# A merge gate as the first unit of tile 0, and all head norms of tile 0 turned by VectorE

## The chip, the cores and the metric

The kernel runs on one core of one Trainium2 chip. The metric is the device time of one execution in microseconds (us), as the median of several runs. Lower is better.

## The reference

The kernel computes one layer of a hybrid decoder block on x of 2048 tokens and 1024 channels, all in float32. Cut to what matters here:

```python
h = rms_norm(x, norm_g)
u = einsum('bsd,dc->bsc', h, w_in)          # 1024 -> 8704 columns
v_c, b_c, c_c, z_c, q, k, v, z_a, gate_logits = split(u)
y_c = b_c * causal_conv3(c_c * v_c) * silu(z_c)
y_a = y_c @ w_conv_out
q, k = rms_norm(q per head of 64), rms_norm(k per head of 64)   # 16 query heads, 4 key heads
o = sliding_window_attention(q, k, v, sinks) * silu(z_a)        # window 128, blocks of 128
y_b = o @ w_attn_out
g_a, g_b = split(sigmoid(gate_logits + gate_b))
out = x + (g_a * y_a + g_b * y_b) @ w_out
```

The queries need an RMS norm per head of 64 channels before the attention, which asks for a sum of squares over those channels. The merge gates g_a and g_b need nothing but h; they are used only when y_a and y_b are merged.

## The kernel before, in words

The 2048 tokens are cut into two tiles of T = 1024 (t = 0 and 1), and each tile into two halves q of 512. Channels lie on the 128 partitions, tokens along the free dimension. A weight matrix is handled in units of 256 output columns: `q0` to `q3` are the queries (one unit is one key head with its four query heads), `cv0` to `cv7` the pairs (conv C, conv v), `b0` to `b3` conv B, `ga0` to `ga3` and `gb0` to `gb3` the merge gates, `z`, `za` the SiLU gates, `ya`, `yb` the two branch projections. `SEQ0` and `SEQ1` are the written-out orders of the units in the two tiles; a `+` joins two units that run interleaved. After tile 1 come eight units of the output projection.

Each float32 operand is split into a high and a low part, and a product is three matmuls (high by high, high by low, low by high) for each of four chunks: 12 matmuls of 128x512. An ordinary unit (`sunit`) is a 2x2x2 block product in seven such products instead of eight; it needs sums of operands (the forms 5, 6, 7 and 4) and sums of weights. The plain unit (`qunit`, kind "P" in the weight plan) takes eight products with the raw operands 1, 2, 8 and 3, so it can start while the sums are still being made. It yields its four results of 128x512 straight in PSUM banks, one after each second product. In the kernel before, `q0` of tile 0 is the one plain unit; it comes first behind the keys and values.

The order of work is written out by hand. Each product is one tick; `run` emits the product of a tick on TensorE and then what was put at that tick with `put(n, f)`. Thus the instruction stream of every engine and DMA queue follows the ticks, and each instruction waits only for the data or the buffer it needs. Tile 0 has 16 ticks for keys and values, then 8 for the plain unit, then 7 for every ordinary unit. `OP_X`, `OP_F`, `OP_S`, `OP_K` and so on hold ticks of the preparation at the front. `AT0` and `AT1` hold the 32 ticks at which the attention blocks (key head j, block b) of a tile begin; each block goes through loads on SP's queue five ticks ahead, scores (TensorE), exponent (ScalarE), normalising and a 32x32 turn (VectorE), a round trip through DRAM on POOL's queue, masks on POOL, values (TensorE) and an output store, over 15 ticks. `STATS_AT` is the tick at which the rows of tile 1's x begin to be loaded (eight transfers of 512 KB on POOL's queue, two ticks apart, `h_stats`, L1372) for tile 1's norm. The unit `z0` of tile 0 and all that follows it keeps its tick.

The norm of the queries (`fin_q`, from L811): each of the four results of a unit is copied to SBUF (L582), scaled and split into `q_h` and `q_l` (`parts`, L850 and L262) and stored to DRAM through POOL's queue (L855). Its sum of squares is taken from a turned copy: with `BY_PE[j]` 1 four TensorE transposes (L708) put tokens on the partitions; with 0 VectorE's STREAM_TRANSPOSE turns the 32x32 blocks. ScalarE squares the turned bank (L782) and VectorE reduces it. After VectorE's turn a head's sum lies in two parts in different partition groups, and `squares_sum` joins them by four ScalarE copies (L802) and four VectorE adds (L804) for a unit. The inverse root of `q0` to `q2` of tile 0 uses a Sqrt activation (`ROOT`, L279). The banks for the turned copies come from one pool of three PSUM banks (`mbank`), shared with the turned keys (`pbk`, L766) and the attention's values (`po`, L1116).

The merge gate (`fin_g`, L1191): one Tanh activation for each result, to be stored to DRAM by SP's queue (L1193).

Of the kernel before, what the change touches and what calls it, by code (L numbers as in the profile page):

```python
# [60 lines left out]
Q_PARTS = [1, 4, 4, 0]  # L61
Q_SUMS = [8, 7, 6, 3]
ROOT = (1, 1, 1, 0)
BY_PE = [1, 1, 1, 0]
OP_X = [1, 1, 1, 6, 7, 7, 8, 11]
OP_P = [3, 2, 3, 4, 4, 4, 5, 6]
OP_L = [7, 8, 6, 6, 8, 7, 9, 7]
# [4 lines left out]
OP_S = [15, 16, 16, 19, 21, 17, 23, 23, 20, 19, 22, 22, 27, 21, 23, 28]  # L72
OP_K = [11, 12, 18, 22, 8, 13, 20, 32, 15, 31, 26, 28, 39, 36]
SEQ0 = (
    "q0 q1 q2 q3 cv0 cv1 cv2 cv3 b0 cv4 cv5 b1 b2 cv6 cv7 b3 ga0 gb2 gb1 ga2 gb0 ga1 gb3 ga3 z0 "
    "z1 z2 z3 za0 za1 za2+za3 ya0+ya1 ya2+ya3 yb0+yb1 yb2+yb3")
SEQ1 = (
    "ga0+ga1 k q0 v q1 q2 cv0 q3 cv1 cv2 b0 cv3 ga3 b1 cv4 cv5 cv6 b2 cv7 gb1 b3 gb3 ga2 gb0 "
    "gb2 z0 z1 z2 z3 za0 za1 za2+za3 ya0+ya1 ya2+ya3 yb0+yb1 yb2+yb3")
STATS_AT = 115  # L80
ORDER = (1, 5, 6, 2, 7, 3, 4)
PAIR_PIECES = ((0, 0), (0, 1), (1, 0), (1, 1), (0, 2), (1, 2), (0, 3), (1, 3))
SUM_AT = {5: 0, 6: 1, 7: 2, 4: 3}
# [10 lines left out]
H_UP = 3  # L94
SUM_WAIT = 6
AT0 = [
    51, 56, 62, 66, 72, 78, 82, 87, 93, 99, 103, 108, 113, 119, 123, 127, 130, 135, 139, 142, 146, 149,
    153, 156, 160, 164, 167, 170, 174, 177, 181, 184]
AT1 = [
    41, 48, 56, 61, 67, 72, 75, 81, 84, 87, 90, 96, 99, 105, 109, 115, 119, 123, 126, 129, 132, 138,  # L100
    141, 144, 147, 150, 154, 157, 161, 164, 168, 174]
# [4 lines left out]
def block_kernel(  # L106
# [37 lines left out]
    def x_bank(name):  # L144
        return ps_x.tile([P, H], F32, tag="x", name=name)
# [385 lines left out]
    def qunit(key, ops, fin):  # L531


        u = unit(key)
        nm = "_".join(str(i) for i in key)
        for q in range(2):
            for i in range(2):
                ps = x_bank(f"Q{nm}_{i}_{q}")
                for p in range(2):
                    force(u, (i, p))  # L540
                    hi, lo = ready[u][i, p]
                    for j in range(KP):
                        b = ops[B_AT[p, q]][j]
                        for k, (w, m) in enumerate(((hi, 0), (hi, 1), (lo, 0))):
                            nc.tensor.matmul(
                                ps, lhsT=w[:, j, :], rhs=b[:, m, :],
                                start=p == 0 and j == 0 and k == 0, stop=p == 1 and j == KP - 1 and k == 2)
                    if p:
                        fin(i, q, ps)
                        live[0] -= 2 * q  # L550
                    yield
# [132 lines left out]
    def run(gen):  # L684
        while True:
            tick[0] += 1
            if next(gen, gen) is gen:
                tick[0] -= 1
                return
            hi, lo = (piece() if tick[0] >= W_FROM else None) or (None, None)  # L690
            if hi:
                hi()

            fs = at.pop(tick[0], [])
            for f in fs[:3]:
                f()
            if lo:
                lo()
            for f in fs[3:]:
                f()  # L700
            ahead_loads()
            vec.some(WOVEN)
# [105 lines left out]
    def fin_q(t, j):  # L808
        by_pe = t == 0 and BY_PE[j]
        ss = small.tile([P, 32 if by_pe else 64], F32, tag="ss" if by_pe else "ss4", bufs=3 if by_pe else 2, name=f"qss{t}_{j}")  # L810
# [629 lines left out]
    for t in range(NT):  # L1440
        def s(key, *srcs):
            plan.append(("S", srcs, key))

        def at_(key, c0):
            s(key, (w_in2, c0), (w_in2, c0 + P))

        if t == 0:
            for i in range(2):
                plan.append(("R", wkv[i * H : (i + 1) * H], ("kv", i)))
        for word in (SEQ0, SEQ1)[t].split():  # L1450
            both_ = word.split("+")
            for name in both_:
                if len(both_) > 1:
                    paired.add(len(plan))
                key, j = name.rstrip("0123456789"), int(name[-1]) if name[-1].isdigit() else None
                if key in ("ya", "yb"):
                    w = w_co if key == "ya" else w_ao
                    s((key, t, j), (w, j * UC), (w, j * UC + P))
                elif key == "cv":
                    s((key, t, j), (w_in2, COL_C + j * P), (w_in2, COL_V + j * P))  # L1460
                elif j is None:
                    at_((key, t), COLS[key])
                else:
                    at_((key, t, j), COLS[key] + j * UC)
                if t == 0 and name == "q0":
                    plan[-1] = ("P",) + plan[-1][1:]
    for n in range(S // P // 2):
        t, c0 = divmod(2 * n * P, T)
# [13 lines left out]
    raw, ops, xs = st["raw"], st["ops"], st["x"]  # L1482
# [171 lines left out]
    for t in range(NT):  # L1654
        ops = state[t]["ops"]
        ys, opa, opb = {}, {}, {}
        t0 = tick[0] + 1 if t else 1
        a0 = t0 + (14 if t else 0)
        attention(t, [a0 + n for n in (AT0, AT1)[t]])

        def unit_of(name, at_of):
            key, j = name.rstrip("0123456789"), int(name[-1]) if name[-1].isdigit() else None
            o = {"ya": opa, "yb": opb}.get(key, ops)
            if key == "k":
                return (key, t), o, fin_k(t)
            if key == "v":
                return (key, t), o, fin_v(t)
            if key == "q":
                fin = fin_q(t, j)
            elif key == "cv":  # L1670
                fin = fin_cv(t, j, ys)
            elif key == "b":
                fin = fin_b(t, j, ys)
            elif key in ("ga", "gb"):
                fin = fin_g(t, int(key == "gb"), j)
            elif key == "z":
                fin = fin_z(t, j, lambda k, q: yd[t][k, :, hs(q)], "z", ("c", t), ycd[t], at_of, nc.sync)
            elif key == "za":
                fin = fin_z(t, j, lambda k, q: od[t][k, :, hs(q)], "za", ("a", t), ocd[t], at_of, nc.gpsimd)
            else:  # L1680
                fin = fin_y(t, int(key == "yb"), j, at_of)
            return (key, t, j), o, fin

        if t + 1 < NT:
            h_stats(t + 1, tick[0] + STATS_AT)
        for word in (SEQ0, SEQ1)[t].split():
            n = tick[0] + 1
            if word == "z0":
                (h_prep if t + 1 < NT else w_prep)(*((t + 1,) if t + 1 < NT else ()), tick[0])
            if word == "za2+za3":  # L1690
                load_set(("c", t), n, opa)
            if word == "ya2+ya3":
                load_set(("a", t), n, opb)
            if word == "yb2+yb3":
                load_set(("h", t + 1) if t + 1 < NT else ("w", 0), n, x_state(t + 1)["ops"])
            names = word.split("+")
            if len(names) > 1:
                paired_units([
                    unit_of(name, lambda e, i=i, n=n: n + 2 * e + i) for i, name in enumerate(names)])
            elif t == 0 and word == "q0":  # L1700
                run(qunit(("q", 0, 0), ops, fin_q(0, 0)))
            else:
                run(sunit(*unit_of(word, lambda e, n=n: n + e)))

# [57 lines left out]
```

## Time and profile before

| | |
|---|---|
| median of 3 runs | 1891.03 us (1890.13 to 2689.12) |
| the profiled execution | 1891.0 us, span 1889.3 us |
| TensorE (PE) busy | 1880.3 us of the span, 8638 matmuls |
| VectorE (DVE) busy | 1540.2 us |
| ScalarE (ACT) busy | 988.9 us |
| GpSimd (POOL) busy | 726.6 us |
| granted TensorE clock | 1.0 |

A row of the profile names engine, line of the kernel, operation, `out<-in` by the program's tile names, shapes and count; then busy time, mean duration, and the idle time before with what ended it. PEld is the load of TensorE's stationary operand and overlaps PE. Matmuls overlap each other, so their rate is read from the distance between starts and not from a duration.

### The profile page before, as it was taken

Reading aid. Unit: us, or ns where it says so; the run is one execution under the profiler, and the core shown is the slowest. Engines: PE = TensorE matmul, PEld = TensorE weight load, DVE = VectorE, ACT = ScalarE, POOL = GpSimd, SP = SyncE. Lnnn points to the kernel's source line nnn. Section 1 sums busy time; section 2 is a strip of 40 time slices with the busy share of each in tenths; the row PEclk is TensorE's granted clock in tenths of the full one; section 3 lists DMA queues with packets and bytes.
Section 4 is the critical chain, followed back from the end, with each engine's and each line's share of the span. In section 5 each row is a group of like instructions: output and inputs, shape, how many; then the busy total and the mean of one; then the engine's idle time right before and its main releaser. Section 6 shows DMA issues by size and latency. Waiting matters only on the chain.

```text
span 1889.3 us, 27890 instructions
## 1 busy us (share of the span) xinstructions
PE 1880.3 (100%) x8638; PEld 1564.8 (83%) x8638; DVE 1540.2 (82%) x2536; ACT 988.9 (52%) x1993; POOL 726.6 (38%) x1038
## 2 busy tenths in 40 slices
PE   9999999999999999999999999999999999999999
PEld 7888888888888888888887888888888888888887
DVE  7989888789878889887588988888888779887654
ACT  7655554567665345435455645556566436444321
POOL 1472454466767111021075445656666311121000
PEclk9999999999999999999999999999999999999999
DMA  8475566689889978899367557768888879989653
GB/s 307 119 216 171 145 177 189 183 247 301 249 250 256 315 266 308 286 282 300 112 181 221 182 172 206 205 165 236 251 237 259 266 245 339 326 270 282 223 173 110
DMA packets 261188, 435.81 MB, mean 231 GB/s; under 512 B 33648, under 2 KB 124784, under 8 KB 261040
## 3 DMA queue, kind: packets, MB, share of 16 engines
q1 hardware_dynamic: 202848, 314.13, 50.6%
q0 software_dynamic: 58048, 119.87, 24.0%
q8 instruction: 69, 1.13, 0.2%
q14 instruction: 79, 0.65, 0.1%
q10 hardware_dynamic: 144, 0.03, 0.0%
HBM read 279.48 MB, written 154.42 MB: 230 GB/s over the span
## 4 chain that ended last, share of the span: by engine, by line
PE 91%; DVE 4%; DMA 3%; issue 1%; POOL 1%; ACT 1%; SPq 0%; POOLq 0%; DVEq 0%; ACTq 0%
PE Y L480 32%; PE Vcv L480 5%; PE Xcv L480 5%; PE s L1027 3%; PE Xz L480 2%; PE Xb L480 2%; PE Vb L480 2%; PE Vga L480 2%; PE Xga L480 2%; PE Vz L480 2%; PE Xza L480 2%; PE Vo L480 2%; PE Xo L480 2%; PE Xyb L480 2%; PE Vyb L480 2%; PE Vza L480 2%
## 5 line engine op out<-in xcount | busy, mean ns | idle before, releaser
L1078 POOL DMA_DIRECT2D x<-fd x256 | 143.8, 609 | 71.7 <-DMA fd<-f 37.1
L1099 POOL TENSOR_SCALAR_AFFINE_SELECT xh<-xh 64x512 fp32r<-64x512 f32 x64 | 66.7, 1042 | 134.8 <-DVE xl L262 98.5
L1051 ACT ACTIVATE p<-s,st,rq 128x128 f32<-128x128 f32 x256 | 113.0, 451 | 3.4 <-DMA fd<-f 2.7
L1071 POOL DMA_DIRECT2D fd<-f x64 | 38.6, 603 | 177.5 <-DVE f L262 162.8
L480 PE MATMUL Xcv<-oph,wcv_ah 128*128 128x512 f32 x256 | 79.1, 390 | 0.0
L1132 POOL DMA_DIRECT2D od<-o x64 | 69.3, 1090 | 21.0 <-ACT wz_d L362 8.0
L855 POOL DMA_DIRECT2D q2d<-q_h x64 | 44.3, 692 | 84.1 <-ACT q_h L850 81.9
L1322 POOL DMA_DIRECT2D md<-thyb x32 | 27.4, 872 | 100.1 <-DVE thyb L262 87.2
L1099 POOL TENSOR_SCALAR_AFFINE_SELECT xl<-xl 64x512 fp32r<-64x512 f32 x64 | 62.9, 983 | 4.4
L1099 POOL TENSOR_SCALAR_AFFINE_SELECT yp<-xl 64x512 fp32r<-64x512 f32 x64 | 55.9, 874 | 3.1
L1099 POOL TENSOR_SCALAR_AFFINE_SELECT yp<-yp 64x512 fp32r<-64x512 f32 x64 | 55.3, 863 | 4.2
L480 PEld LDWEIGHTS Xcv<-oph,wcv_ah 128*128 128x128 f32 x256 | 47.6, 188 | 9.4
L262 DVE SCALAR_TENSOR_TENSOR y<-u,cols,y 128x512 f32<-128x512 f32 x64 | 51.5, 804 | 3.7 <-ACT y L1161 2.5
L262 DVE TENSOR_TENSOR opa<-ina,opa 128x512 fp32r<-128x512 f32 x56 | 36.2, 686 | 21.6 <-ACT opa L297 21.4
L262 DVE TENSOR_TENSOR p<-p,st 128x512 f32<-128x512 f32 x64 | 49.2, 769 | 2.8
L1051 ACT ACTIVATION_READ_ACCUMULATOR p<-s,st,rq 128x1 f32 x256 | 51.1, 199 | 0.0
L362 ACT CAST wcv_sh<-wcv_raw 128x1024 fp32r<-128x1024 f32 x16 | 16.8, 1052 | 63.4 <-DVE wcv_raw L262 63.4
L480 PE MATMUL Xcv<-oph,wcv_al 128*128 128x512 f32 x128 | 49.9, 390 | 0.0
L855 POOL DMA_DIRECT2D q2d<-q_l x64 | 44.1, 689 | 13.6 <-DVE q_l L262 8.9
L262 DVE STREAM_TRANSPOSE f<-p 128x512 f32<-128x512 f32 x64 | 45.4, 710 | 2.6 <-DVE p L262 0.2
L262 DVE TENSOR_TENSOR opc<-inc,opc 128x512 fp32r<-128x512 f32 x56 | 36.1, 686 | 13.8 <-ACT opc L297 11.5
L480 PE MATMUL Y<-oph,wcv_d 128*128 128x512 f32 x192 | 46.4, 390 | 0.0
(774 smaller groups left out, 6594.4 us busy)
## 6 DMA issues: line engine op xcount, KB each, us to landing
wcv_raw<-in_w_in SPq DMA_DIRECT2D x32, 512.0 KB, 4.2
q<-q2d SPq DMA_DIRECT2D x64, 256.0 KB, 4.8
v<-vd SPq DMA_DIRECT2D x128, 128.0 KB, 4.4
fd<-f POOLq DMA_DIRECT2D x64, 256.0 KB, 3.8
x<-fd POOLq DMA_DIRECT2D x256, 64.0 KB, 3.5
gd<-th SPq DMA_DIRECT2D x64, 256.0 KB, 3.3
wq_raw<-in_w_in SPq DMA_DIRECT2D x16, 512.0 KB, 5.1
q2d<-q_h POOLq DMA_DIRECT2D x64, 128.0 KB, 3.6
```

Source lines behind the costliest of these rows:

```text
L262: r = f(*args, **kw)
L362: return (lambda: nc.scalar.copy(hi, src), lambda: vec.tensor_tensor(out=lo, in0=src, in1=hi.bitcast(F32), op=ALU.subtract))
L480: nc.tensor.matmul(ps, lhsT=w[:, j, :], rhs=b[:, m, :], start=start and j == 0 and i == 0, stop=j == KP - 1 and i == 2, skip_group_check=n ...
L855: nc.gpsimd.dma_start(q2d[t][j][half, q * 2 * HB : (q + 1) * 2 * HB, i, e, :], src[HALVES[e]].bitcast(F32).rearrange("p (b x) -> p b x", x ...
L1027: nc.tensor.matmul(to, lhsT=w, rhs=x_, start=n == 0, stop=n == 2, skip_group_check=h == 1)
L1051: nc.scalar.activation(out=p[:, i, :], in_=sg[:, i, HD : 3 * HD], func=AF.Exp, bias=st[:, 1, i : i + 1], scale=rv[:, i // 2, i % 2 : i % 2 ...
L1071: nc.gpsimd.dma_start(fd, f)
L1078: nc.gpsimd.dma_start(x[QUADS[k]], src[k])
L1099: nc.gpsimd.affine_select(out=d4, in_=s4, pattern=[[0, 2], [-32 * sg, 2], [0, G], [-sg, 32]], compare_op=ALU.is_gt if prev else ALU.is_ge, ...
L1132: put(tick[0] + ADD_WAIT, lambda: nc.gpsimd.dma_start(to, o[UH].rearrange("p c e q -> p (c e) q"), accum_op=ALU.add))
L1322: nc.gpsimd.dma_start(md[t][k, :, hs(q)], m, accum_op=ALU.add)
```

## The change

`ga0` (the first 256 columns of merge gate a) trades its late place in tile 0 for the first one and becomes the plain unit; `q0` becomes an ordinary unit, second in line. `q1`, `q2`, `q3`, the eight `cv` and the four `b` units of tile 0 thus come 7 ticks later than before; `gb2` and all that follows keep their ticks. `BY_PE` becomes zero for all four query units of tile 0, so that VectorE turns what TensorE turned in `q0`, `q1` and `q2`. The attention steps of tile 0 start 7 ticks later, the shift shrinks along the list, and the last two places are unchanged. The loads of tile 1's rows start 7 ticks later.

```diff
-BY_PE = [1, 1, 1, 0]
+BY_PE = [0, 0, 0, 0]
 SEQ0 = (
-    "q0 q1 q2 q3 cv0 cv1 cv2 cv3 b0 cv4 cv5 b1 b2 cv6 cv7 b3 ga0 gb2 gb1 ga2 gb0 ga1 gb3 ga3 z0 "
+    "ga0 q0 q1 q2 q3 cv0 cv1 cv2 cv3 b0 cv4 cv5 b1 b2 cv6 cv7 b3 gb2 gb1 ga2 gb0 ga1 gb3 ga3 z0 "
     "z1 z2 z3 za0 za1 za2+za3 ya0+ya1 ya2+ya3 yb0+yb1 yb2+yb3")
-STATS_AT = 115
+STATS_AT = 122
 AT0 = [
-    51, 56, 62, 66, 72, 78, 82, 87, 93, 99, 103, 108, 113, 119, 123, 127, 130, 135, 139, 142, 146, 149,
-    153, 156, 160, 164, 167, 170, 174, 177, 181, 184]
+    58, 63, 69, 72, 78, 84, 88, 92, 98, 104, 108, 113, 117, 123, 127, 131, 133, 138, 142, 145,
+    148, 151, 155, 158, 162, 165, 168, 171, 175, 177, 181, 184]
...
-                if t == 0 and name == "q0":
+                if t == 0 and name == "ga0":
                     plan[-1] = ("P",) + plan[-1][1:]
...
-            elif t == 0 and word == "q0":
-                run(qunit(("q", 0, 0), ops, fin_q(0, 0)))
+            elif t == 0 and word == "ga0":
+                run(qunit(*unit_of(word, None)))
```

## The prediction

> **What bounds the kernel now.** I read the head of the page first, then TensorE's own waits.
>
> ```profile
> span 1889.3 us, 27890 instructions
> PE 1880.3 (100%) x8638; PEld 1564.8 (83%) x8638; DVE 1540.2 (82%) x2536; ACT 988.9 (52%) x1993; POOL 726.6 (38%) x1038
> PEclk9999999999999999999999999999999999999999
> PE 91%; DVE 4%; DMA 3%; issue 1%; POOL 1%; ACT 1%; SPq 0%; POOLq 0%; DVEq 0%; ACTq 0%
> ```
>
> TensorE has a matmul in flight for 1880.3 of 1889.3 us, at full granted clock in every slice, and 91% of the chain that ended last is its own. A busy TensorE is not yet one at its rate, so the waits come next (TensorE's alone, longest first).
>
> ```profile
> PE Y L1496 <- DVE zero L181: 1.5, 1, 1.5
> PE ptr L614 <- DVE rtok L607: 1.3, 1, 1.3
> PE Vq L480 <- DVE wq_sl L262: 0.7, 1, 0.7
> PE Vv L480 <- DVE wv_sl L262: 0.4, 1, 0.4
> PE Vq L480 <- ACT wq_sh L362: 0.3, 1, 0.3
> PE Y L480 <- DVE th L262: 0.3, 1, 0.3
> ```
>
> These six sum to 4.5 us, of which 2.8 lie in the first two, ahead of every unit. So there is nearly nothing to win in waits: the time changes by TensorE work taken away or by waits made. The profiled execution took 1891.0 us, 1.7 outside its span, and equals the median of the runs (1891.03); I sum against 1891.0.
>
> **What TensorE loses.** The matmuls of the units don't change in number: one plain unit (96) and the rest ordinary (84) before and after, only another name in the plain place. What goes is the turning of `q0` to `q2`.
>
> ```profile
> L708 PE MATMUL ptq<-ident,q_t x48: 270/272/273, 83.9 to 139.8; 128*128 128x128 f32 x48
> 90.27 0.60 PE L708 MATMUL ptq<-ident,q_t 128*128 128x128 f32 x4
> 90.62 0.71 PE L480 MATMUL Vq<-oph,wq_th 128*128 128x512 f32 x2
> 91.17 0.40 PE L480 MATMUL Vq<-oph,wq_tl 128*128 128x512 f32 x1
> 93.46 0.39 PE L480 MATMUL Y<-oph,wq_d 128*128 128x512 f32 x1
> 142.67 0.61 PE L480 MATMUL Vcv<-oph,wcv_sh 128*128 128x512 f32 x2
> 145.39 0.39 PE L480 MATMUL Y<-oph,wcv_sh 128*128 128x512 f32 x1
> ```
>
> The first row is the 48 transposes, four for each of 12 results. Their duration of 272 ns overlaps, so I take the distance of starts instead. A product of 12 matmuls with nothing between takes 145.39 - 142.67 = 2.72 us (227 ns a matmul). With a group of four transposes ahead of it, it takes 93.46 - 90.27 = 3.19 us: 0.35 for the group and 0.12 until the stream is back at its rate. A group costs 0.47 us, all of it on the path, because TensorE has nothing else to put there. Twelve groups: **-5.6 us**.
>
> The Trainium skill, VectorE: DVE Perf Modes, "The three transpose paths" and the rules behind it, says to turn 128x128 blocks on TensorE if the result may lie in PSUM, as it does here, at 390 ns a block against 311 on VectorE. By that figure 48 blocks would be an estimated 18.7 us of TensorE; in this stream they are 5.6, because transposes follow each other every 0.1 us.
>
> The front has one more stall that may go.
>
> ```profile
> 80.34 0.60 PE L766 MATMUL pbk<-ident,k_n 128*128 128x128 f32 x4
> 80.70 1.03 PE L480 MATMUL Y<-oph,wq_sh 128*128 128x512 f32 x2
> 81.56 0.39 PE L480 MATMUL Y<-oph,wq_sl 128*128 128x512 f32 x1
> ```
>
> Behind the turned keys two matmuls take 81.56 - 80.70 = 0.86 us, where the two at 90.62 take 0.55: 0.3 us of waiting for an operand that VectorE makes. Three `q_l` splits of the first queries run on VectorE before this moment, and they move away with `q0`. I take **-0.3 us**, between 0 (the operand is late for another cause) and -1.7, the 4.5 us above less the first two rows.
>
> **What VectorE and ScalarE get.** The price of the other way to turn stands in the trace, since `q3` and tile 1 use it already.
>
> ```profile
> L262 DVE STREAM_TRANSPOSE ptq<-q_t x20: 683/718/721, 145.0 to 1068.6; 128x512 f32<-128x512 f32 x20
> L804 DVE TENSOR_TENSOR q_b<-qss,q_g x20: 171/182/189, 160.0 to 1076.8; 32x32 f32<-32x32 f32 x20
> L802 ACT COPY q_g<-qss x20: 213/218/219, 158.7 to 1075.6; 32x32 f32<-32x32 f32 x20
> ```
>
> Twelve turns by 0.718 are 8.6 us on VectorE, and three times four adds by 0.182 are 2.2: 10.8 us. ScalarE gets twelve copies by 0.218, 2.6 us. Whether that is hidden is read from the stretches of one unit each: span; then busy time of PE, PEld, DVE, ACT, POOL; granted clock; DMA share; GB/s.
>
> ```profile
> 53.10:74.90 21.80, 21.80 (x98) 18.02 (x97) 21.45 (x40) 15.16 (x29) 7.44 (x12) 1.00 0.21 55
> 74.90:96.50 21.60, 21.55 (x104) 17.60 (x103) 21.53 (x34) 14.29 (x25) 10.65 (x17) 1.00 0.74 209
> 96.50:117.90 21.40, 21.40 (x107) 17.80 (x106) 18.26 (x37) 12.04 (x22) 15.71 (x24) 1.00 0.67 191
> 117.90:139.80 21.90, 21.90 (x110) 18.15 (x109) 17.55 (x31) 13.66 (x24) 15.46 (x24) 1.00 0.83 233
> 139.80:159.60 19.80, 19.80 (x93) 16.49 (x92) 19.08 (x35) 11.18 (x21) 8.68 (x13) 1.00 0.69 212
> ```
>
> These are the places of `q0`, `q1`, `q2`, `q3` and `cv0`; after the change `ga0`, `q0`, `q1`, `q2` and `q3` stand there. VectorE is full in the first two (42.98 of 43.40 us) with the operand sums, but the turns don't fall there: `Q_SUMS` puts `q0`'s first turn 9 ticks behind its result, near tick 37, which is in the third stretch. The last three have 63.10 - 54.89 = 8.2 us of idle VectorE. The 10.8 us meet this and a lighter `ga0`: its results go from PSUM through one ScalarE Tanh each, with no split and no VectorE instruction, while every `q` result needs a split. `cv0`'s VectorE work also leaves the stretch, as do the first attention blocks. So I cost the turns at **0**. If that cover were missing, the bound from above is the excess, 10.8 - 8.2 = 2.6 us; I see no way to a gain. On TensorE nothing waits for the turned bank any more, except that turned keys share the three banks with it.
>
> ScalarE trades four copies out of PSUM for four Tanh in the first stretch.
>
> ```profile
> L582 ACT COPY q_t<-Qq 128x512 f32<-128x512 f32 x4 | 2.3, 581 | 4.2 <-PE Qq L545 4.2
> L1191 ACT ACTIVATE th<-Xga,hbias x8: 687/690/692, 402.9 to 1368.4; 128x512 f32<-128x512 f32 x8
> L279 ACT ACTIVATE q_t<-q_ms x3: 229/229/231, 111.5 to 147.6; 128x32 f32<-128x32 f32 x3
> L1048 ACT ACT_TABLE_LOAD x3 | 3.8, 1283 | 0.1
> ```
>
> A Tanh takes 0.69 against 0.58, 0.4 us in all. But it now stands between Sqrt activations: those of the keys and, at L279, of the queries come after it. Table loads occur where the function changes to Exp (L1048), at 1.283 us each with 0.1 us idle before all three. Tanh at L1191 has none of its own among the Exps. So I count two more loads: Sqrt to Tanh at tick 18, and back to Sqrt later; the third, to Exp, is there already. That is 2.6 us of ScalarE in stretches where it idles 6.6 of 21.8 and more, and the bank that the Tanh empties is not needed again for two products, 5.4 us. On the path: **0**, at most 2.6 if both loads stood ahead of something that TensorE waits for. The Trainium skill, ScalarE: Activation LUTs, "Table sets: the hidden batching unit", says tanh is in exp's set and sqrt in another; the trace agrees on the first, with no load at L1191, and the rule speaks against this order. With the drain that it states, a switch is 2.66 us, and two would be an estimated 5.3 instead of 2.6.
>
> **Queues.** The four gate stores (256 KB each) move to the first stretch, where the DMA share is 0.21. On SP's queue they wait for the Tanh, and weight loads stand behind them. SP is held there anyway:
>
> ```profile
> SPq L340 <- DVE wq_sl L262: 122.1, 6, 34.6
> 75.77 8.14 SPq L340 DMA_DIRECT2D wq_raw<-in_w_in  x2
> ```
>
> The next weight load waits 34.6 us for its buffer and issues at 75.77, by which time the plain unit's last Tanh is about done; cost 0 to 0.7. POOL's queue gets the query stores 7 ticks later, and the attention that reads them comes 7 ticks later too: 0.
>
> **The attention and the row loads.** The first blocks move with the queries they read; up to the last places the list is squeezed from 133 ticks to 126, 5.6% denser. The row loads move one unit on, about 20 us.
>
> ```profile
> L1372 POOL DMA_DIRECT2D x<-in_x x8: 533/568/590, 400.2 to 446.5; - x8
> 440.00:460.00 20.00, 19.73 (x94) 16.25 (x94) 17.96 (x41) 15.53 (x39) 11.14 (x17) 1.00 1.02 324
> 453.80 3.06 PE L480 MATMUL Y<-oph,wgb_d 128*128 128x512 f32 x12 [0.27 <-DVE th L262]
> ```
>
> Seven ticks of 2.72 us later, less the 5.6 saved ahead of them, they lie in about 414 to 460 and take in the stretch whose DMA share is full, where TensorE already waited 0.27 us for VectorE. What keeps this small is that `ga0` left the same part of tile 0, with its 1 MB of stores, its Tanhs and its adds. I take **+0.4 us**, one or two waits of that size; below, the bound is the present wait gone (it is among the 1.7 above); above, the rival below.
>
> Sum: 1891.0 - 5.6 - 0.3 + 0.4 = **1885.5 us**. With no new wait and all the small ones gone it is 1891.0 - 5.6 - 1.7 = 1883.7; I put the low end at 1883.5.
>
> **Rivals.** *Slower: the attention's loads become late.* The second row is for 380 to 500 us, the first for the whole kernel (KB each, median us to landing).
>
> ```profile
> kq<-kd SPq DMA_DIRECT2D x56, 128.0 KB, 4.2
> kq<-kd SPq DMA_DIRECT2D x8, 128.0 KB, 5.8
> ```
>
> A key load takes 1.6 us longer here. If the row loads and the denser blocks lengthen it once more by as much, and the five ticks of lead don't cover it, the scores come late and TensorE waits. The row loads span 46 us, some four or five blocks; with 1.6 us for each the wait is 6.4 to 8.0 us, and 1891.0 - 5.9 + 7.2 = 1892.3. It decides once the new waits pass 5.9 us. For it: DMA share 1.02, and the row at 453.80. Against: one wait of 0.27 us in the same traffic today. *VectorE becomes the bound at the front.* The excess of 2.6 us and part of the table loads reach TensorE: 1885.5 + 2.6 to 1885.5 + 5.2, say 1888.7. For it: 42.98 of 43.40 us busy just ahead. This is how the skill's rule in VectorE: DVE Perf Modes would come out right here. *The transposes are not saved.* If the stream only closed up to meet another bound, the time would stay at 1891; against it stands the 0.47 us beside every group with no other wait near.
>
> **Chances.** Forecast with its own range 1883.5 to 1887: 0.72. Front bound by VectorE: 0.12. Late attention: 0.09. Not saved: 0.07. The range of 8 in 10 takes the forecast and the second case and stops short of the last two: 1883.5 to 1890.5. A measurement here tells about 2% (38 us) from no change, and every case lies far inside that: within 2% 0.96, slower by over 2% 0.02 for late blocks that pile up, faster 0.02.
>
> **What would show it.** Right: no `ptq` matmuls at L708 under `q_t`, 8590 matmuls; a query unit takes 84 x 0.227 = 19.0 us and 0.5 more for each group of turned keys in it; two table loads more, one at L1191; TensorE's waits still about 5 us. Wrong: waits of TensorE on `oph`, weights or `pbk` between 75 and 165 us (the front), or on `s`, `po` or `Y` between 400 and 560 us (the attention).

## The result, and the profile after

The changed kernel takes 1910.39 us, the median of its runs (1908.51 at best), against 1891.1 for the kernel before beside it: 1.0101 times as long, 95% interval 1.009 to 1.0112. That is 19.3 us slower, inside the 2% that counts as no change here, and outside the predicted range of 1883.5 to 1890.5. One run of each kernel took some 2690 us at a far lower clock and stands in these medians; without it they are 1909.37 and 1891.03, so that differences from 1910.39 below can be 1 us too large. The profiled execution took 1908.51 us; its span is 17.5 us longer than that of before.

The head of the page, and the shares of the chain that ended last:

```profile
span 1906.8 us, 27837 instructions
PE 1882.6 (99%) x8590; PEld 1562.3 (82%) x8590; DVE 1547.0 (81%) x2551; ACT 993.5 (52%) x2006; POOL 726.9 (38%) x1038
PE 70%; issue 11%; DVE 6%; DMA 6%; POOL 5%; ACT 1%; SPq 1%; POOLq 0%; DVEq 0%; ACTq 0%
```

TensorE has 48 matmuls fewer, as intended, and yet 2.3 us more busy time, since some of its matmuls ran at half clock (below). Its idle time went from 9.0 to 24.2 us. The chain is TensorE's own for 70% where it was for 91%. TensorE's longest waits (total, times, longest one):

```profile
PE Y L480 <- DVE q_t L262: 3.5, 1, 3.5
PE s L1027 <- ACT p L1051: 3.5, 2, 2.0
PE Vgb L480 <- ACT wgb_sh L362: 1.9, 1, 1.9
PE po L1116 <- POOL xl L1099: 1.5, 2, 0.8
...
PE Vga L480 <- DVE wga_sl L262: 1.1, 1, 1.1
```

The first is at the front, in `q3`. Those on `s`, `Vgb`, `po` and `Vga` lie between 370 and 565 us, in the second half of tile 0's attention. Both places were named in the prediction as those that would show it wrong.

To see how much each place took, I cut both spans at the starts of units. First the five units at the front. Before, their stretches stand in the prediction's table: 106.50 us from 53.10 to 159.60, 106.45 of them busy. After, with the same columns, `ga0` and `q0` together, then `q1`, `q2`, `q3`:

```profile
51.83:93.59 41.76, 41.76 (x189) 34.56 (x188) 39.17 (x66) 27.39 (x48) 7.92 (x13) 1.00 0.40 117
93.59:114.14 20.55, 19.87 (x90) 16.08 (x88) 16.28 (x27) 12.48 (x19) 15.11 (x23) 1.00 0.73 209
114.14:133.65 19.51, 19.51 (x89) 16.16 (x88) 16.50 (x32) 11.61 (x23) 13.28 (x20) 1.00 0.77 227
133.65:158.31 24.66, 21.15 (x86) 16.75 (x85) 19.60 (x37) 14.56 (x26) 16.41 (x25) 0.93 0.60 166
```

These sum to 106.48: nothing was gained where 5.9 us were expected. After, TensorE is idle for 4.19 us of them against 0.05, 3.51 of it in the last row, where the mean clock is 0.93, which is 24.66 x 0.07 = 1.7 us lost. 4.1 + 1.7 = 5.8 us: about what the transposes and the front's old stall had freed was given back, most of it (3.5 + 1.7) in one place. Next, `z0` and what follows keep their ticks. Its first row, before and then after:

```profile
L480 PE MATMUL Xz<-oph,wz_ah x128: 387/389/474, 568.4 to 1495.9; 128*128 128x512 f32 x128
```

```profile
L480 PE MATMUL Xz<-oph,wz_ah x128: 389/389/477, 586.1 to 1513.4; 128*128 128x512 f32 x128
```

From the end of those five units to `z0` lie 19 units in both kernels. They took 568.4 - 159.6 = 408.8 us before and 586.1 - 158.3 = 427.8 after, 19.0 more. From `z0` to the end it is 1320.9 and 1320.7, and the first unit starts 1.3 us earlier (51.83 against 53.10). That start moved between 51.7 and 53.2 in the experiments too, whatever was changed, so I count it as scatter. -1.3 + 0.0 + 19.0 - 0.2 = 17.5, the difference of the spans. There are two questions, then: why the front gave its gain back, and why the late part of tile 0 lost 19 us.

**The stall at the front, row by row.** TensorE's timeline of the changed kernel (start, duration, and in brackets the idle time before and what ended it):

```profile
149.97 0.39 PE L480 MATMUL Vq<-oph,wq_tl 128*128 128x512 f32 x1
153.86 4.60 PE L480 MATMUL Y<-oph,wq_d 128*128 128x512 f32 x12 [3.51 <-DVE q_t L262]
158.31 0.63 PE L480 MATMUL Xcv<-oph,wcv_ah 128*128 128x512 f32 x2
```

The last product of `q3` needs the bank `Y`, which VectorE frees with the sum `q_t<-Y,s5q`. VectorE's timeline of the same moment, and then ScalarE's:

```profile
148.55 0.75 DVE L262 SCALAR_TENSOR_TENSOR q_l<-q_t,gqk,q_h 128x512 fp32r<-128x512 f32 x1 [1.53 <-ACT q_h L850]
...
149.48 0.69 DVE L262 STREAM_TRANSPOSE ptq<-q_t 128x512 f32<-128x512 f32 x1
...
151.44 0.75 DVE L262 SCALAR_TENSOR_TENSOR q_l<-q_t,gqk,q_h 128x512 fp32r<-128x512 f32 x1 [1.20 <-ACT q_h L850]
...
153.12 0.68 DVE L262 TENSOR_TENSOR q_t<-Y,s5q 128x512 f32<-128x512 f32 x1
```

```profile
150.20 0.58 ACT L782 ACTIVATE ptq<-ptq 128x512 f32<-128x512 f32 x1 [1.18 <-DVE ptq L262]
150.69 0.71 ACT L850 ACTIVATE q_h<-q_t,gqk 128x512 fp32r<-128x512 f32 x1
153.84 0.72 ACT L850 ACTIVATE q_h<-q_t,gqk 128x512 fp32r<-128x512 f32 x1 [2.44 <-DVE q_t L262]
```

Read across the two. ScalarE's square at L782 stands in its stream behind other work and waits 1.18 us for VectorE's turn. Behind the square stands the next `q_h`, with nothing to wait for but its place. VectorE's `q_l` waits 1.20 us for that `q_h`. Behind `q_l` stands the sum that frees `Y`, and that is what TensorE waits for. Neither engine is full (VectorE idles 1.53 and 1.20 us here, ScalarE 1.18 and 2.44). Each waits in order for the other.

### The profile page after: what moved, and what is told of

Read it like the earlier page. It is cut to its first block, busy times and chain, and to the rows that moved or that the text cites. A ratio compares the mean times of both kernels' runs of the same rounds, so it can differ in the third digit from the quotient of the medians.

```text
span 1906.8 us, 27837 instructions
## 1 busy us (share of the span) xinstructions
PE 1882.6 (99%) x8590; PEld 1562.3 (82%) x8590; DVE 1547.0 (81%) x2551; ACT 993.5 (52%) x2006; POOL 726.9 (38%) x1038
## 4 chain that ended last, share of the span: by engine, by line
PE 70%; issue 11%; DVE 6%; DMA 6%; POOL 5%; ACT 1%; SPq 1%; POOLq 0%; DVEq 0%; ACTq 0%
PE Y L480 24%; PE Xcv L480 4%; PE Vcv L480 4%; PE Vo L480 2%; PE Xo L480 2%; PE Vz L480 2%; PE s L1027 2%; PE po L1116 2%; PE Xz L480 2%; PE Vya L480 2%; PE Xya L480 2%; PE Vgb L480 2%; PE Vb L480 2%; PE Xgb L480 2%; PE Xb L480 2%
## 5 line engine op out<-in xcount | busy, mean ns | idle before, releaser
L1132 POOL DMA_DIRECT2D od<-o x64 | 69.8, 1098 | 16.8 <-DMA od<-o 16.2
L262 DVE TENSOR_TENSOR xl<-x,xh 128x512 fp32r<-128x512 f32 x64 | 43.7, 682 | 9.1 <-DMA lows<-kd 5.3
L1027 PE MATMUL s<-lows,kq 128*128 128x384 f32 (+2 forms) x128 | 44.1, 344 | 3.5 <-ACT p L1051 3.5
```

Source lines behind the costliest of these rows:

```text
L262: r = f(*args, **kw)
L1027: nc.tensor.matmul(to, lhsT=w, rhs=x_, start=n == 0, stop=n == 2, skip_group_check=h == 1)
L1132: put(tick[0] + ADD_WAIT, lambda: nc.gpsimd.dma_start(to, o[UH].rearrange("p c e q -> p (c e) q"), accum_op=ALU.add))
```

## The experiments

The kernel before ran beside every one of them, at 1890.6 to 1891.2 us; ratios are against those runs, with their 95% intervals, and need not equal the quotient of the two medians.

### The front: VectorE's time, or its hand-over to ScalarE

My first theory was the reading above, a hand-over that comes too late within a product. The rival was that VectorE simply has too much to do. The turns alone, in the kernel before:

```diff
-BY_PE = [1, 1, 1, 0]
+BY_PE = [0, 0, 0, 0]
```

> The kernel before with one edit: all four query units of tile 0 are turned by VectorE (BY_PE all zero), order and attention as before. Theory 1 (the 48 transposes are pure TensorE time and the turns are hidden, as the prediction had it): 1891.1 - 5.6 = 1885.5 us, 8590 matmuls, no new TensorE wait over 1 us ahead of 165 us. Theory 2 (the turns on VectorE make the stall seen at 150 to 158 us in the changed kernel, 3.5 us of waiting and some 1.7 us of half clock): the gain is eaten, 1890 to 1891 us, with a wait of that kind at the end of the third or fourth query unit.

1898.06 us, 1.0038 (1.0024 to 1.0052): 7.1 us slower. From `q0` to `cv0` it took 92.7 us against 86.7. TensorE's longest waits, which were not there before:

```profile
PE Y L480 <- DVE q_t L262: 2.3, 1, 2.3
PE Y L480 <- DVE Vq L262: 2.1, 1, 2.1
PE pbk L766 <- DVE qss L262: 1.6, 1, 1.6
```

All three name VectorE. So the turns by themselves cost more than the transposes they replace. In the changed kernel they cost less (at the end of this section); the lighter `ga0` may absorb part there, but no run isolates it. Two kernels then separate time from order. The first keeps TensorE's transposes and gives VectorE twelve reductions more, 0.67 to 0.69 us each, which nobody waits for:

```diff
+                    vec.tensor_reduce(
+                        out=halo.rearrange("p k c -> p (k c)"), in_=qt.rearrange("p (h d) -> p h d", d=32),
+                        axis=AX.X, op=ALU.add)
```

> The kernel before, TensorE turning as before, with twelve extra VectorE instructions that nobody waits for: a sum over 128x512 into the still unused halo columns, one behind each TensorE turn of the first three query units of tile 0 (the output is not changed). Theory 1 (VectorE's time is what is missing: the same 8 us that the turns took make the front stall): waits of TensorE between 95 and 150 us as in the kernel with turns alone, 1897 to 1903 us. Theory 2 (what costs is that VectorE, ScalarE and VectorE again hand each turned copy on, each in its order, not VectorE's time): 1890 to 1893 us.

1893.04 us, 1.0013 (1.0004 to 1.0022): +1.9 us for some 8 us of VectorE work. That is a little less than the 10.8 us of turns and adds, so this run alone does not rule out VectorE's time. The second is the kernel with the turns alone, but the turned copy goes to a buffer in SBUF and ScalarE squares it one tick later:

```diff
-                    pt = mbank(f"pt{nm}")
+                    pt = slot([P, HB, P], F32, f"pt{nm}") if t == 0 else mbank(f"pt{nm}")
...
+                if t == 0:
+                    put(tick[0] + 1, lambda: square(pt))
+                else:
+                    square(pt)
```

> The kernel with turns alone (order and attention as before, VectorE turns all queries of tile 0), changed so that the turned copy lies in SBUF and ScalarE's square of it comes one tick behind VectorE's turn instead of right behind it; the reduction follows one tick later. VectorE and ScalarE do the same work. Theory 1 (VectorE's time is missing): as with turns alone, 1896 to 1900 us. Theory 2 (the hand-over from VectorE to ScalarE and back inside a tick stalls the two in-order engines in turn): the stalls go and the transposes' 5.6 us are saved, 1885 to 1889 us. Theory 3 (the shared PSUM banks are the cause): the wait on pbk goes, the two others stay, 1893 to 1896 us.

1892.67 us, 1.0007 (0.9998 to 1.0017). The same turns, nearly the same time on each engine, one tick of distance: 5.4 of the 7.1 us come back. Over the whole kernel ScalarE's square waited 31.0 us in 24 waits for the turn with the turns alone, and 12.0 in 11 here. The edit does a second thing, though: it takes the turned copy out of the three shared PSUM banks. The wait on `pbk` (1.6 us) went with that, and no run separates the two. `q0` to `cv0` now takes 84.6 us, 2.1 less than before the change. What is left appears one unit later:

```profile
PE Vcv L480 <- DVE wcv_sl L262: 1.9, 1, 1.9
PE Y L480 <- DVE Vq L262: 1.4, 1, 1.4
PE Y L480 <- DVE q_t L262: 1.2, 1, 1.2
```

`cv0` waits for its weights' low part, which VectorE makes late, and takes 23.7 us instead of 19.8. So the hand-over, with the bank, is the larger part. Waits on what VectorE makes late remain: with the order mended, the freed 5.6 us still don't reach the end. The same edit in the changed kernel:

> The changed kernel with the turned copies of tile 0 in SBUF and ScalarE's square one tick behind VectorE's turn (the reduction a tick later), as in the run with turns alone. Theory 1 (the hand-over inside a tick makes the front stall of the changed kernel too): the wait of 3.5 us at 154 us and its half clock go, 1904 to 1907 us; the late waits stay. Theory 2 (the front stall of the changed kernel is another one, from the query stores or VectorE's time): 1909 us or more.

1906.47 us, 1.0081 (1.0066 to 1.0096), 3.9 us under the changed kernel by the medians; the intervals just overlap. From `ga0` to `cv0` it took 103.2 us where the changed kernel took 106.5. Its wait on `q_t` fell from 3.5 to 1.2, and the 1.9 on `wcv_sl` appeared here too.

The other half, everything but the turns: the changed kernel with `BY_PE = [1, 1, 1, 0]`.

> The changed kernel with one edit: TensorE turns the first three query units again (BY_PE 1, 1, 1, 0); order, attention places and row loads stay changed. Theory 1 (the loss is made by order and attention, the transposes are worth 5.6 us): 1910.4 + 5.6 = 1916 us. Theory 2 (the turns on VectorE make the front stall of 5.2 us): 1910.4 + 5.6 - 5.2 = about 1911 us, with no wait of several us at 150 us.

1911.1 us, 1.0107 (1.0092 to 1.0122), the time of the changed kernel. With the new order, turning by VectorE or by TensorE makes no clear difference (0.7 us), so the turns cost there some 4 to 5 of the 5.6 us that they should save. The rest of the change costs 20.2 us by itself.

### The late part: places, rows or the gate

The start of the row loads put back, in the changed kernel:

```diff
-STATS_AT = 122
+STATS_AT = 115
```

> The changed kernel with one edit: the row loads of tile 1 start at tick 115 from the first unit as before, not 122. Theory 1 (the row loads, issued late by POOL's queue behind the denser attention, hold ScalarE and so TensorE between 415 and 565 us): most of the late loss of some 18 us returns, 1893 to 1898 us, and no wait on a gate's weights at 440 us. Theory 2 (the denser attention itself is late, with or without row loads): within 4 us of the changed kernel, 1906 to 1911 us.

1905.79 us, 1.0085 (1.007 to 1.0101): 4.6 us come back by the medians, but the intervals overlap, and the profiled execution was the slowest of the four (1911.32 us). Its trace shows the wait on `wgb_sh` gone and others in its place (3.0 us on `th`, 5.3 on scores), and not the gain. The attention's places alone, in the kernel before, with nothing else of the change:

```diff
-    51, 56, 62, 66, 72, 78, 82, 87, 93, 99, 103, 108, 113, 119, 123, 127, 130, 135, 139, 142, 146, 149,
-    153, 156, 160, 164, 167, 170, 174, 177, 181, 184]
+    58, 63, 69, 72, 78, 84, 88, 92, 98, 104, 108, 113, 117, 123, 127, 131, 133, 138, 142, 145,
+    148, 151, 155, 158, 162, 165, 168, 171, 175, 177, 181, 184]
```

> The kernel before with one edit: the attention places of the changed kernel (later at the start, 5.6% denser, the same end); order, turns and row loads as before. Theory 1 (the row loads are needed for the loss): at most 3 us over the kernel before, 1891 to 1894 us. Theory 2 (the denser attention by itself makes TensorE wait on scores, values and late weights between 360 and 565 us): 1900 to 1909 us.

1904.06 us, 1.0069 (1.0054 to 1.0084): +13.1 us, the largest part of all. TensorE's waits:

```profile
PE s L1027 <- ACT p L1051: 5.8, 4, 2.2
PE Y L480 <- DVE th L262: 1.9, 1, 1.9
PE Vga L480 <- DVE wga_sl L262: 1.6, 1, 1.6
```

Scores wait for the bank that ScalarE's exponent of the block before still reads. The trace also shows why that exponent is late. The longest of the four waits, in VectorE's, ScalarE's and TensorE's rows:

```profile
528.50 0.57 DVE L262 TENSOR_TENSOR st<-cols,st 128x4 f32<-128x4 f32 x1
```

```profile
531.59 1.05 ACT L362 CAST wgb_sh<-wgb_raw 128x1024 fp32r<-128x1024 f32 x1 [4.08 <-DVE wgb_raw L262]
...
534.48 0.47 ACT L1051 ACTIVATE p<-s,st,rq 128x128 f32<-128x128 f32 x1
```

```profile
535.10 0.60 PE L1027 MATMUL s<-lows,kq 128*128 128x384 f32 x1 [2.23 <-ACT p L1051]
```

What the exponent needs from VectorE is there at 529.07 us, but ScalarE stands 4.08 us at a weight split ahead of it, and the last of the four exponents starts only at 534.48. The other two long waits (1.78 and 1.42 us) follow in the same way a Tanh of a gate, at which ScalarE stood 4.74 and 4.61 us for TensorE's product. In the kernel before, ScalarE mostly came first: between 360 and 570 us it waited 20.7 us for what the exponent needs, against 15.1 here and 9.4 in the changed kernel. So the places decide on which side of the gates' work a block's exponent falls.

Which places of the list do it? Three kernels cut it: the late start caught up within the first six places; only the last 15 places of the new list; and the late start caught up by the 14th place. All three otherwise have the old list.

```diff
-    51, 56, 62, 66, 72, 78, 82, 87, 93, 99, 103, 108, 113, 119, 123, 127, 130, 135, 139, 142, 146, 149,
+    58, 61, 65, 69, 74, 79, 82, 87, 93, 99, 103, 108, 113, 119, 123, 127, 130, 135, 139, 142, 146, 149,
```

> The kernel before with the first six attention places of tile 0 later by 7, 5, 3, 3, 2 and 1 ticks (58, 61, 65, 69, 74, 79) and all others as before: the attention starts as late as in the changed kernel but catches up at once. Theory 1 (the loss of 13 us with the changed places comes from the later, denser part between 400 and 560 us): 1890 to 1893 us. Theory 2 (any late start costs): 1898 us or more.

1896.84 us, 1.0033 (1.002 to 1.0046): +5.7 us. The stall went with the crowding: one wait of 3.1 us on VectorE's `b` at 240.8 us, in the unit where the blocks catch up, and none of the late ones.

```diff
+    51, 56, 62, 66, 72, 78, 82, 87, 93, 99, 103, 108, 113, 119, 123, 127, 130, 138, 142, 145, 148, 151,
+    155, 158, 162, 165, 168, 171, 175, 177, 181, 184]
```

> The kernel before with the first 17 attention places as before and the last 15 as in the changed kernel (3 to 0 ticks later). Theory 1 (the last 15 places, between 400 and 560 us, are by themselves too dense for the units beside them): 1899 to 1905 us, with the waits on scores and gates as with all places moved. Theory 2 (the blocks ahead carry a backlog into that part): 1890 to 1894 us.

1899.17 us, 1.005 (1.0035 to 1.0065). Of the fifteen blocks three stand where they stood; the other twelve, moved by one to three ticks each, cost 8.0 us.

```diff
+    58, 63, 69, 72, 78, 84, 88, 92, 98, 104, 108, 112, 116, 119, 123, 127, 130, 135, 139, 142, 146, 149,
```

> The kernel before with the attention starting as late as in the changed kernel, but catching up in places 12 to 16 (112, 116, 119, 123, 127), so that the last 16 places are the old ones. Theory 1 (only local crowding costs, and there is room where the row loads and gates are not): 1890 to 1893 us, no wait on scores between 440 and 560 us. Theory 2 (the backlog of the later start must be paid somewhere): 1896 us or more, with a new wait between 300 and 400 us.

1893.96 us, 1.0016 (1.0007 to 1.0025): +3.2 us for the whole late start, if the last 19 places stay what they were. So a late start is cheap if it is caught up in the right places; the later places are not free to move.

What makes a crowded block slow? One candidate is the work on POOL, which masks each block. The kernel before with the new places and without three of the four masks, in both tiles (it leaves out part of what the attention has to mask):

```diff
-        keep(xh[UH], xh[UH], False)
-        keep(y[LH], y[LH], True)
...
-        keep(xl[UH], xl[UH], False)
```

> The kernel before with the changed kernel's attention places, and three of the four masks that GpSimd sets on each turned block left out (only the one that also copies is kept), in both tiles: some 2.7 us of GpSimd less for each block, and its queue free sooner for the round trip's transfers. Theory 1 (the late blocks wait for GpSimd's queue, which holds masks, transfers and stores in one order): most of the 13 us return, 1891 to 1896 us. Theory 2 (VectorE or ScalarE is what the denser blocks lack): 1900 us or more.

1899.53 us, 1.005 (1.0034 to 1.0066): by the medians 4.5 of the 13 us go with the masks and the rest stays. The intervals overlap and the profiled execution took 1905.29 us, so this part is not certain. Another is the lead of the key and query loads, one tick less with the same new places:

```diff
-            put(n - 5, step("l", lambda g, j=j, b=b: att_load(t, j, b)))
+            put(n - 5 + (t == 0), step("l", lambda g, j=j, b=b: att_load(t, j, b)))
```

> The kernel before with the changed kernel's attention places (1904 us), and the loads of queries and keys of tile 0's attention four ticks ahead of the scores instead of five, so that these tiles live a tick less. Theory 1 (buffers are short): faster, 1894 to 1900 us. Theory 2 (the transfers are late): slower, 1908 us or more, with waits on q, kq or lows. Theory 3 (neither): 1902 to 1906 us.

1903.54 us, 1.0073 (1.0058 to 1.0088): no change beside 1904.06, though two waits on a load (second row) appeared in TensorE's list:

```profile
PE s L1027 <- DVE p L262: 3.0, 1, 3.0
PE s L1027 <- DMA lows<-kd: 2.9, 2, 2.3
```

They took the place of others. The blocks are not paced by these loads.

### Buffers

The attention's tiles come from one pool of 19 slots. That the denser blocks run out of slots was my next theory. One slot less, in the kernel before:

```diff
-    big = ctx.enter_context(tc.tile_pool(name="big", bufs=19))
+    big = ctx.enter_context(tc.tile_pool(name="big", bufs=18))
```

> The kernel before with 18 instead of 19 buffers in the pool of 2 KB tiles that the attention's q, k, v, p, f, x and o tiles, the gates and the query copies take in turn. Theory 1 (the buffers are what the denser attention lacks: the next tile waits for the reader of the one 19 places back, on any engine): 1897 us or more, with waits of TensorE between 400 and 560 us like those of the changed kernel. Theory 2 (the engines' and queues' order alone): 1890 to 1893 us.

1913.63 us, 1.0116 (1.0099 to 1.0132): +23.0 us. The pool is short indeed, but the cost is in another place. `z0` starts only 4.9 us later (573.3 against 568.4), and the largest loss stands behind it, in the branch projections and the gates:

```profile
573.30:800.00 226.70, 218.20 (x954) 179.19 (x954) 180.01 (x255) 101.18 (x166) 59.79 (x93) 0.98 0.82 277
```

8.5 us idle, where the same stretch behind `z0` had 0.3 before, and 226.7 x 0.02 = 4.5 us of clock. The opposite test, in the changed kernel, does with nine slots a block instead of ten (the low part is written over the returned block):

```diff
-        xh, xl = slot([P, G, P], F32R, f"xh{nm}"), slot([P, G, P], F32R, f"xl{nm}")
+        xh, xl = slot([P, G, P], F32R, f"xh{nm}"), pt
...
```

> The changed kernel with the low part of each returned attention block written over the block itself, so that a block takes nine of the 19 buffers in turn instead of ten; every instruction, order and place is as in the changed kernel. Theory 1 (the buffers are what the denser places lack): the waits between 400 and 565 us shrink, 1895 to 1903 us. Theory 2 (the order on the engines and queues and the round trip alone): 1907 to 1912 us.

1912.9 us, 1.0106 (1.0084 to 1.0129): no gain. The waits on `s`, `Vgb` and `Vga` are there as in the changed kernel, and none is shorter (4.7, 2.8 and 2.3 us). And all steps of tile 0's blocks behind the round trip (split, low part and masks, values, output, sum) one tick later, which gives the round trip 2.7 us more and holds the slots longer:

```diff
-            put(n + X_, step("x", lambda g, j=j, b=b: att_turn(t, j, b, g["b"])))
+            put(n + X_ + (t == 0), step("x", lambda g, j=j, b=b: att_turn(t, j, b, g["b"])))
```

(and so for the low part, the values, the output and the sum)

> The changed kernel with all steps of tile 0's attention behind the round trip (splitting, masks, values, output) one tick later, so that ScalarE, which takes the returned block in its order, has 2.7 us more until it must wait for the transfer. Theory 1 (ScalarE and GpSimd standing ahead of a late round trip make the late waits): 1899 to 1905 us. Theory 2 (tiles kept a tick longer make it worse: the buffers are short): 1912 us or more. Theory 3 (neither): 1908 to 1912 us.

1923.51 us, 1.0174 (1.0156 to 1.0191), 13 us worse than the changed kernel:

```profile
PE po L1116 <- POOL xl L1099: 4.2, 5, 1.3
...
PE po L1116 <- POOL yp L1099: 2.6, 2, 1.9
```

More time for the round trip does not help: TensorE's waits for POOL's masks grew from 2.3 us in the changed kernel to 6.8. Slots are scarce in this kernel, but with one less in use for each block the waits stayed, so they don't seem to be what the late part of the change waits for.

### Putting the pieces together

The changed kernel with the later square, the list that is caught up by the 14th place, and the old start of the row loads:

> The changed kernel with three edits: the square one tick behind the turn, the attention catching up by place 17 as in the run just above, and the row loads at their old tick. Theory 1 (the losses are the hand-over and the crowded last places, and both are local): 1886 to 1892 us. Theory 2 (moving the merge gate to the front itself costs late, since the other units then lie a unit later beside the same blocks): 1895 us or more, with waits between 400 and 560 us.

1899.01 us, 1.0039 (1.0025 to 1.0053). That is 11.4 us better than the change, and still 8.3 slower than before. The same list and the same start of rows with TensorE's transposes in place of the later square, so that only the gate in front and the late start are left of the change:

> The changed order with everything else as in the run that caught up by place 17: TensorE turns the first three query units, row loads at the old tick, the same attention places. It differs from that run (1894 us) by the merge gate in front alone. Theory 1 (the order by itself is free): 1892 to 1896 us. Theory 2 (the other units lying one unit later beside the same blocks costs): 1898 us or more, by a wait near 430 us.

1898.36 us, 1.0039 (1.0025 to 1.0054). Against the late start alone (+3.2) the gate in front costs 7.7 - 3.2 = 4.5 us. Its profiled execution, 4.6 us above the median, shows one such loss: TensorE waits 4.28 us for scores, and the chain of waits (start, length, what) leads back to a row load:

```profile
420.13 7.52 DMA x<-in_x
...
427.74 0.37 ACT x L603
...
428.88 0.94 ACT wgb_ah L362
...
429.85 1.24 DVE wgb_al L262
...
431.13 1.83 PE s L1027 x6
```

ScalarE's norm of the rows of tile 1 waits for their load, a gate's weight split stands behind it on ScalarE, its low part follows on VectorE, and TensorE has the scores queued behind. The changed kernel shows the same picture. Its row loads, and ScalarE behind them:

```profile
L1372 POOL DMA_DIRECT2D x<-in_x x8: 553/584/1029, 432.2 to 474.2; - x8
```

```profile
439.86 1.06 ACT L603 ACTIVATE x<-x 128x1024 f32<-128x1024 f32 x1 [7.30 <-DMA x<-in_x]
...
441.48 1.03 ACT L362 CAST wgb_sh<-wgb_raw 128x1024 fp32r<-128x1024 f32 x1
```

The first load went out at 432.2 us against 400.2 before, 32 us later, where a unit of seven ticks takes 21.5 us on average there before (408.8 us for 19), and ScalarE stood still for 7.30 us for it. `wgb_sh` is the one that TensorE waited 1.9 us for. Last, the nine-slot edit on the first of these two kernels:

> The changed kernel with all that gave time back: the square one tick behind the turn, the attention catching up by place 17, the row loads at their old tick (1899 us so far), and the low part written over the returned block (one buffer less for each block). Theory 1 (the stall of 4 us at 431 us is a wait for a buffer): 1888 to 1893 us. Theory 2 (it is the round trip that ScalarE stands ahead of): 1896 to 1900 us.

1899.03 us, 1.004 (1.0025 to 1.0055): nothing, again.

## Why the prediction was wrong, point by point

**The transposes: right in size.** No `ptq` under `q_t` is left on TensorE and the matmuls are 8590. Unit `q2` took 19.51 us, where 19.0 and 0.5 for a group of turned keys were forecast. With the hand-over mended, the stretch from `q0` to `cv0` fell under that of before by 2.1 us even with 1.4 and 1.2 us of waits in it, 4.7 together. Most of the 5.6 us was there to be had in the front, though not at the end.

**The turns at 0: the step that failed at the front.** I set 10.8 us of work against 8.2 us of idle VectorE and called the excess the upper bound. That compares amounts. The bound that mattered is a time limit: `Y` must be free within the next product, 2.72 us, and on the way there VectorE and ScalarE wait for one another in order. Measured, the turns alone cost +7.1 us net where -5.6 was due, about 12.7 against the bound of 2.6. In the changed kernel, with its new order, they cost some 4 to 5 (1910.4 with the turns, 1911.1 with the transposes, where 5.6 more were due). 8 us of VectorE work without the hand-over cost 1.9. The hand-over was visible in the trace of before, where ScalarE's square waited 14 times for VectorE's turn, 16.2 us in all; the prediction doesn't take it up. The rival "VectorE becomes the bound at the front" had the right engine, but its price, an excess in busy time, was too small for the same reason. The rule in the Trainium skill, VectorE: DVE Perf Modes, "Rules for kernel authors", that a 128x128 transpose belongs on TensorE if the result may lie in PSUM, comes out right here. Its figures are not the cause: the group of four costs 0.47 us in this stream.

**The front stall, -0.3: right.** Behind the turned keys the same two matmuls now take 79.93 - 79.39 = 0.54 us, where they took 0.86:

```profile
79.39 0.71 PE L480 MATMUL Y<-oph,wq_sh 128*128 128x512 f32 x2
79.93 0.40 PE L480 MATMUL Y<-oph,wq_sl 128*128 128x512 f32 x1
```

The first two units together fell from 43.40 to 41.76 us, which is this and the three groups of transposes that stood in them.

**The table loads: right.** Two more, of 1283 ns each, one at L1191 (56.59 us) and one at L279 (97.69 us), and neither ahead of something that TensorE waited for: TensorE did not idle from 51.83 to 93.59 us, and its next wait ended at 97.60, before the second load.

The Trainium skill, ScalarE: Activation LUTs, "What ACT_TABLE_LOAD costs", adds a drain of about 1.38 us to the 1.28 of a load. The trace agrees with the load and does not show the drain: the Tanh at L1191 starts at 57.88 us, its load at 56.59.

**The attention and the row loads, +0.4: the large miss.** It measured 19.0 us. This is the second step that failed, and the larger one. I took the size of a wait of before, 0.27 us, and one or two of them, since the density rises by only 5.6%. The runs show that the price does not follow the mean density. The new places alone cost 13.1 us, twelve of them moved by one to three ticks 8.0, and the same late start with the last 19 places kept 3.2. The old list stands at spacings that fit the units around it, and a shift of some ticks puts a block's exponent behind a gate's weight split or Tanh on ScalarE, as the rows of that run show. The row loads add 4.6 (by medians whose intervals overlap), the gate in front 4.5. Taken from medians, 3.2 + (13.1 - 3.2) + 4.6 + 4.5 = 22.2 for everything but the turns, where that kernel measured 20.2. The parts add up to within 2 us, which is partly chance, since they come from different kernels and each is uncertain by 2 to 3 us.

**The rival "late attention".** It named the place (400 to 500 us), and waits on `s` and `po` came there. It had a chance of 0.09 and a price of 7.2 us, and neither was enough. Its mechanism, key loads that land later, is not what happened: between 380 and 500 us the key loads of 128 KB took 5.2 us to land in the changed kernel, where they took 5.8 before, and one tick less of their lead changed nothing. What the traces show is ScalarE's exponent holding the scores' bank because ScalarE stands in order behind a gate's work or a row load, and waits for POOL's masks. How much of the 19 us is each stays open. The masks may be about a third of the cost of the places; one tick less of the loads' lead and one slot less in use changed nothing, and I have no run that isolates the order on ScalarE.

**What I left out altogether** is that a stall can cost more than its length. In the balance of the whole span, idle time grew by 15.2 us and the mean clock of 0.997 is worth 1906.8 x 0.003 = 5.7; less 5.6 for the transposes that is 15.3, and the remaining 2 us of 17.5 are not accounted for (the clock is rounded to 0.001, which alone is up to 1 us).

No version came out faster than the kernel before. The nearest was the turns with the later square, without the rest of the change (1892.67, its interval reaches 1); with the gate in front the best is 1898.36.

## What to carry to other kernels

Work that moves to an engine with idle time is hidden only if each of its hand-overs comes in time. Follow the in-order streams from the moved instruction to the next bank that the busy engine needs, and compare that latency with the length of one product; idle shares say nothing of it. Put a tick between a producer and a consumer on another in-order engine, and they wait less for each other (5.4 us here, the freed bank included). A schedule with places written out by hand isn't described by its mean density: keep the spacings that are known to fit and move only as many steps as the change needs.

## What the runs showed of the hardware

Some short stalls of TensorE are followed by about 3 us at half clock, and others are not. Four stalls of the changed kernel, each with the stretch behind it (same columns as above; the clock is the third from the end):

```profile
150.00:155.00 5.00, 1.49 (x6) 0.91 (x5) 2.98 (x9) 1.93 (x3) 5.00 (x8) 0.98 0.74 200
155.00:160.00 5.00, 5.00 (x17) 3.96 (x16) 4.90 (x9) 2.86 (x4) 3.58 (x6) 0.68 0.72 188
440.00:444.00 4.00, 1.61 (x7) 0.71 (x6) 1.23 (x1) 4.00 (x8) 1.97 (x4) 1.00 0.64 148
444.00:448.00 4.00, 4.00 (x13) 3.25 (x14) 2.63 (x6) 3.95 (x7) 0.84 (x2) 0.61 1.01 351
512.00:516.00 4.00, 2.41 (x13) 1.59 (x11) 3.93 (x5) 2.73 (x6) 3.88 (x5) 1.00 0.00 0
516.00:520.00 4.00, 4.00 (x12) 2.84 (x10) 3.00 (x8) 2.92 (x12) 2.24 (x4) 0.57 0.83 223
538.00:542.00 4.00, 1.95 (x12) 1.59 (x11) 2.36 (x5) 3.71 (x13) 2.21 (x4) 1.00 0.60 98
542.00:546.00 4.00, 4.00 (x21) 3.43 (x21) 3.61 (x6) 3.89 (x7) 0.58 (x1) 1.00 0.60 197
```

Idle for 3.51, 2.39 and 1.59 us in the first three, TensorE then lost 5 x 0.32 = 1.6, 4 x 0.39 = 1.6 and 4 x 0.43 = 1.7 us to the clock. The product at 153.86 shows the same in starts: 4.45 us to the next one instead of 2.72. So there a stall of 1.6 us cost 3.3, and one of 3.5 cost 5.1. In the fourth, idle for 2.05 us, the clock stayed at 1.00. So it did after the stall of 3.10 us in the kernel whose attention catches up in the first six places (1.00 from 241 to 245 us). The length of a stall alone does not decide. The Trainium skill, TensorE: Matmul & The Clock Gate, "What's actually happening", states half clock after an idle window of about 3.4 us. The first stall agrees; the second and third are shorter, and the clock fell all the same, the third after two waits of 0.8 us with matmuls between. Which stalls cost double can't be told from these runs, so the clock has to be read behind each.
